# A transformer step on one core: the layout of an intermediate in DRAM, the place of 24 row gathers, and the place of eight gate products

## The chip, the cores and the metric

The kernel runs on one core of a Trainium2 chip. The metric is the device time of one execution in microseconds (us). The engines named below are PE (matrix products, with PEld for its weight loads), DVE (VectorE), ACT (ScalarE), POOL (GpSimd, which here issues the indirect gathers) and SP (SyncE, which issues nearly all other transfers).

## What is computed

One decoder layer in float32 on 512 prompt tokens and 64 decode tokens of width 1024: attention and a state-space branch are mixed by two gates, projected and normalised; then follows a layer of 16384 one-neuron experts (PEER) of which each token uses 8 x 16. The places that matter here:

```python
mix = jax.nn.sigmoid(ga) * (a @ w_attn_proj) + jax.nn.sigmoid(gb) * (s @ w_ssm_proj)
x = layer_norm(DN_ALPHA * x + mix @ w_out, ln1_g, ln1_b)
x = layer_norm(DN_ALPHA * x + peer(x, ...), ln2_g, ln2_b)
x = x + jax.nn.sigmoid(x @ ple_w_gate) * (p @ ple_w_proj)
# peer, one block of 128 tokens: 16 expert numbers idx and weights g for each of 8 heads
ue = u_tab[idx]
ve = v_tab[idx]
h = jax.nn.gelu(jnp.einsum('td,thkd->thk', xb, ue), approximate=False)
return jnp.einsum('thk,thkd->td', (g * h), ve)
```

## The kernel before

The tokens are five blocks: block 0 holds the 64 decode tokens, blocks 1 to 4 the prompt. Two groups run through the mixing one after the other: A (blocks 0 and 1, until about 397 us) and B (blocks 2 to 4, 384 token columns).

**PEER in two ways.** Blocks 2, 3 and 4 are computed densely over all 16384 experts, which are 128 columns of 128. `first` (L1202) makes 50 columns of activations: `up` (L1125) loads 512 KB of `u_t`, splits them on ACT (`uh`) and DVE (`ul`) into two parts and runs 24 matmuls (L1138) into `gl`; 48 of the results go to DRAM (`Hd`). Beside the columns runs `side`: the top-k of a block and then its `grid` (L1143), which turns the 128 weights of each token into a dense grid. A grid takes eight steps of 16 tokens; in each, DVE makes the tiles `o`, `eq`, `oa` and in most steps `ob` (ACT makes the others), PE multiplies them (L1169, L1170), ACT copies PSUM into `Gs`, and every second step a 2 MB `Gs` tile goes to `Gg` in DRAM (L1174), four times in a grid; there are two `Gs` tiles (`GSB`). `dense` (L1228) then walks over the 128 columns, the other 78 with their `up`, the last 50 with `gl` read back from `Hd`. Each column reads `v_tab` (512 KB), each fourth column four columns of the grid (`G<-Gg`, L1258, 768 KB), multiplies grid and activation (`wt`), splits both and runs the products of L1278. While the last 50 columns run, `w_gate` is loaded (`fr`) for the end of the program.

**Rows.** Blocks 1 and 0 are computed by gathers: `gathered_rows` (L1071) takes, for each of 128 (64 for block 0, packed) choices, one row of `u_tab` for every token, multiplies it with x on DVE and sums (`scr`, L1085), then the same with `v_tab` into `acc` (L1094). These are 384 rows: 192 of u, 192 of v. Each is one indirect gather of 512 KB issued by POOL (L1075) into one of four buffers `g`, and one DVE instruction. DVE keeps the rows in program order. The order is: u and v of block 1, then u and v of block 0. The gather for a row is issued when a buffer is free, so four run ahead of DVE.

**What sets the order.** Work is written as generators. At fixed places the code calls `pull(n)`, which adds n to an account and puts as many whole rows there: `PULL1` after each column of `first`, `PULL3` and `PULL4` in `dense`, `P0`, `P1`, `P2`, `P3`, `P4`, `PG` in group B's steps. What is left at the end of the program is done by `pull(1000)` ahead of block 0's layer norm. A scheduler then orders the instructions of each engine, within the bounds of data and buffers.

**Group B's mixing.** After the GLU of the state-space branch come `gate1` (L545: the eight gates of the second branch, 8 x 8 matmuls of L404, kept in `g1`), `mix0` (L561: attention times `w_ap` by L411, added into `mixB` by DVE), `mix1` (L575: state-space result times `w_sp`, times its gate, plus `mixB`), then `out`, `ln1`, `peerq`. Beside `mix0` DVE finishes the top-k of block 0 (tiles `eq`, `PF`, `ef`, `idx`), on which the first gathers of block 0 rest; the rows that are done there are block 1's.

**The end.** Block 0 comes last: after its last `acc` row a matmul folds it (L1100), DVE adds and normalises it, and PE runs its last gate products (L1373).

## Time and profile before

| | us |
|---|---|
| runs of the kernel before (3) | 1905.57, 1906.43, 1909.03; median 1906.43 |
| profiled execution, its own time | 1906.19 |
| its span in the profile | 1904.2 |
| group B from the GLU's end to `out` | 397 to 487 |
| `first`, 50 columns with three grids | from about 629, the last 242 us of it 690 to 932 |
| `dense`, 78 columns with `up` | 932 to 1563 |
| `dense`, last 50 columns | 1563 to 1799 |
| the end | 1799 to 1904.2 |

In the rows below, a table of windows gives for each stretch its length, the busy time of each engine with its number of instructions, the granted clock of TensorE as a share of full speed, the mean busy share of 16 DMA engines, and GB/s. A row of grouped instructions gives line, engine, operation, out<-in, count, then busy us and mean ns of one, then the idle time of the engine ahead of them and what ended it. A row of the timeline gives start, length, engine and line, and in brackets the idle time just ahead. Times are of one execution, from the start of its span.

### The profile page before, as it was taken

How to read it: one execution, taken by the hardware profiler on the slowest of the kernel's cores; microseconds unless marked ns; L12 is line 12 of the kernel's file. 1: busy time of each engine (PE TensorE's matmuls, PEld its weight loads, DVE VectorE, ACT ScalarE, POOL GpSimd, SP SyncE). 2: the span in 40 equal slices, each digit the busy share in tenths (PEclk: the TensorE clock that was granted, in tenths of full speed). 3: DMA queues.
4: the chain of work that ended last, by engine and by line, in shares of the span. 5: the costliest groups of instructions: out<-in, count | busy, mean ns of one | idle time of the engine just before them, and what ended most of it. 6: DMA issues, size and time to landing. Idle time of an engine off the chain costs nothing.

```text
span 1904.2 us, 26616 instructions
## 1 busy us (share of the span) xinstructions
PE 1789.2 (94%) x9506; PEld 1538.8 (81%) x9506; DVE 1474.5 (77%) x2969; ACT 770.0 (40%) x1145; POOL 576.4 (30%) x425
## 2 busy tenths in 40 slices
PE   7889999997999989999999999999999998999946
PEld 5768987756769678889999999999999996788835
DVE  7642344897889998968688888888888877988884
ACT  2115452241243259687733333333333324433311
POOL 4210000024431000000055555555555552332250
PEclk9899999998999989999999999999999999999978
DMA  7925464158794447577899999999999989999672
GB/s 215 305 91 171 148 221 167 55 190 330 272 358 168 136 159 283 196 282 267 310 375 367 348 335 350 336 352 333 353 337 342 342 285 410 392 353 355 215 235 85
DMA packets 211076, 515.45 MB, mean 271 GB/s; under 512 B 33536, under 2 KB 103184, under 8 KB 208880
## 3 DMA queue, kind: packets, MB, share of 16 engines
q1 hardware_dynamic: 144496, 301.68, 45.1%
q0 software_dynamic: 56160, 204.78, 29.3%
q10 hardware_dynamic: 10288, 7.30, 1.3%
q8 instruction: 74, 1.21, 0.2%
q14 instruction: 58, 0.48, 0.1%
HBM read 463.31 MB, written 51.89 MB: 271 GB/s over the span
## 4 chain that ended last, share of the span: by engine, by line
PE 63%; DVE 16%; DMA 9%; issue 6%; ACT 4%; POOL 1%; SPq 0%; ACTq 0%; DVEq 0%; POOLq 0%
PE psB L1278 11%; PE psA L1278 11%; PE psA L1138 11%; PE psB L1138 9%; PE psA L404 6%; PE psA L411 3%; DVE eq L217 3%; DMA g<-u_tab,idx 3%; ACT Gs L211 2%; PE psB L404 2%; DMA fr<-w_gate 2%; DMA g<-v_tab,idx 1%; POOL g L1075 1%; DVE scr L1085 1%; PE psA L648 1%
## 5 line engine op out<-in xcount | busy, mean ns | idle before, releaser
L1075 POOL DMA_INDIRECT g<-u_tab,idx x192 | 263.3, 1371 | 856.1 <-DVE scr L1085 571.2
L1075 POOL DMA_INDIRECT g<-v_tab,idx x192 | 274.2, 1428 | 315.3 <-DVE acc L1094 259.3
L1085 DVE SCALAR_TENSOR_TENSOR scr<-g,x 128x1024 bf16<-128x1024 f32 x192 | 234.6, 1222 | 38.3 <-DMA g<-u_tab,idx 36.7
L1094 DVE SCALAR_TENSOR_TENSOR acc<-g,hh,acc 128x1024 f32<-128x1024 f32 x190 | 243.6, 1282 | 15.9 <-DMA g<-v_tab,idx 13.9
L214 ACT ACTIVATE uh<-ur 128x1024 fp32r<-128x1024 f32 x120 | 127.2, 1066 | 138.3 <-PE psA L1138 70.2
L217 DVE TENSOR_TENSOR ul<-ur,uh 128x1024 fp32r<-128x1024 f32 x120 | 146.2, 1220 | 43.9 <-ACT uh L214 29.9
L214 ACT ACTIVATE vh<-vr 128x1024 fp32r<-128x1024 f32 x128 | 136.0, 1063 | 105.1 <-PE psB L1278 90.0
L214 ACT ACTIVATE wh<-wt 128x384 fp32r<-128x384 f32 x128 | 67.1, 524 | 239.2 <-PE psB L1278 221.8
L217 DVE TENSOR_TENSOR vl<-vr,vh 128x1024 fp32r<-128x1024 f32 x128 | 156.2, 1220 | 5.6 <-ACT vh L214 5.6
L1278 PE MATMUL psA<-vh,wh 128*128 128x512 f32 x384 | 150.4, 392 | 8.6 <-ACT wh L214 8.6
L217 DVE TENSOR_TENSOR wl<-wt,wh 128x384 fp32r<-128x384 f32 x128 | 71.6, 559 | 105.7 <-PE psB L1278 96.7
L1278 PE MATMUL psA<-vl,wh 128*128 128x512 f32 x384 | 150.9, 393 | 0.1
L1278 PE MATMUL psB<-vl,wh 128*128 128x512 f32 x384 | 150.6, 392 | 0.0
L1278 PE MATMUL psB<-vh,wh 128*128 128x512 f32 x384 | 150.2, 391 | 0.0
L1278 PE MATMUL psB<-vh,wl 128*128 128x512 f32 x384 | 149.9, 390 | 0.0
L1278 PE MATMUL psA<-vh,wl 128*128 128x512 f32 x384 | 149.5, 389 | 0.0
L1138 PE MATMUL psA<-xh,uh 128*128 128x384 f32 x648 | 135.3, 348 | 8.0 <-ACT uh L214 8.0
L404 PE MATMUL psB<-xTB,w 128*128 128x384 f32 x400 | 134.2, 492 | 5.9 <-ACT ev L214 5.9
L1138 PEld LDWEIGHTS psA<-xh,uh 128*128 128x128 f32 x648 | 115.7, 193 | 14.6 <-ACT uh L214 11.0
L1138 PE MATMUL psA<-xh,ul 128*128 128x384 f32 x648 | 127.1, 338 | 0.0
L1138 PE MATMUL psA<-xl,uh 128*128 128x384 f32 x648 | 126.9, 337 | 0.0
L404 PEld LDWEIGHTS psB<-xTB,w 128*128 128x128 f32 x400 | 76.3, 193 | 56.6 <-ACT ev L214 6.5
(366 smaller groups left out, 3625.2 us busy)
## 6 DMA issues: line engine op xcount, KB each, us to landing
ur<-u_t SPq DMA_DIRECT2D x128, 512.0 KB, 6.8
vr<-v_tab SPq DMA_DIRECT2D x128, 512.0 KB, 6.4
G<-Gg SPq DMA_DIRECT2D x33, 768.0 KB, 8.2
Gg<-Gs SPq DMA_DIRECT2D x12, 2048.0 KB, 7.4
w<-w_in SPq DMA_DIRECT2D x42, 512.0 KB, 5.2
w<-w_q SPq DMA_DIRECT2D x32, 512.0 KB, 5.3
Hd<-gl SPq DMA_DIRECT2D x48, 192.0 KB, 2.2
gl<-Hd SPq DMA_DIRECT2D x48, 192.0 KB, 5.6
```

The lines of the kernel that those rows point to most:

```text
L211: S.activation(out, in_, fn, **k)
L214: S.activation(out, in_, AF.Copy)
L217: return (e or V).tensor_tensor(out, a, b, op=op)
L404: T.matmul(out, w[:, k, :], x[:, k, :], start=(k == 0), stop=(k == kc - 1))
L411: T.matmul(out, a[:, k], b[:, k], start=f and k == 0, stop=l and k == kc - 1)
L648: T.matmul(p[bi][:n], a[:, k + i, c0:c0 + n], b[:, i], start=f and i == 0, stop=e and i == 1)
L1075: G.indirect_dma_start(out=t, out_offset=None, in_=I[tab], in_offset=bass.IndirectOffsetOnAxis(ap=IDX[bi][:, i:i + 1], axis=0))
L1085: pin(V.scalar_tensor_tensor(scr, t, 1.0, X1[bi], op0=mult, op1=mult, accum_out=hh[:, i:i + 1]))
L1094: pin(V.scalar_tensor_tensor(acc, t, hh[:, i:i + 1], acc, op0=mult, op1=add))
L1138: T.matmul(p, w[:, c * 128:c * 128 + 128], z[:, c], start=f and c == 0, stop=l and c == 7)
L1278: T.matmul(y[b][hf], x[:, bs], z[:, hf * 512:hf * 512 + 512], start=f, stop=l)
```

## The change

Four things change.

1. `Gg` is laid out in DRAM as [128, 32, 12, 128] in place of [12, 128, 128, 32]. A write of `Gs` (2 MB) now consists of 4096 pieces of 512 bytes, where it was 128 pieces of 16 KB; a read of four columns (768 KB) consists of 128 pieces of 6 KB, where it was 1536 pieces of 512 bytes.
2. `PULL1` goes from 0.25 to 0.75, `P0` from 1 to 0.75, `P1` from 0.5 to 1.5, and the 16 rows of `gate1` (`PG`) fall away.
3. `gate1` is gone; `mix1` computes each gate of B itself, as it did for group A, between its products.
4. `up` is cut into `up_parts` (load and split) and `up` (matmuls); in `first` the parts of the next column stand ahead of the matmuls of this one.

```diff
--- before.py
+++ after.py
@@ -37,7 +37,7 @@
 E0 = 50
 EB, KB, TB = 1, 1, 1
 BQ, ABG, AB0, AB1, AB2 = 2, 0, 1, 1.5, 2
-P0, P1, P2, P3, P4, PG = 1, 0.5, 3, 2, 2, 2
+P0, P1, P2, P3, P4 = 0.75, 1.5, 3, 2, 2
 YFIRST = True
 QK0, QK1 = (4, 0, 1), (2, 3)
 SIDE = 2
@@ -54,7 +54,7 @@
 T0, T1, T2 = 0.5, 1, 1
 LATE = 0
 AHEAD = 3
-PULL1, PULL3, PULL4, PULL5 = 0.25, 3, 1, 2
+PULL1, PULL3, PULL4, PULL5 = 0.75, 3, 1, 2
 
 
 
@@ -542,13 +542,6 @@
                             act(g.mx[:, n], g.mm(g.ln.wload(I["w_in"][10 + n]), g.xT, 8), AF.Sigmoid)
                             yield
 
-                    def gate1(g, xp):
-
-                        g.g1 = xp.tile([128, 8, g.N], FP, name="g1", tag="xh")
-                        for n in range(8):
-                            act(g.g1[:, n], g.mm(g.ln.wload(I["w_in"][18 + n]), g.xT, 8), AF.Sigmoid)
-                            yield
-
                     def half(g, w, n, x):
 
                         o = n % 2 * 4
@@ -586,11 +579,8 @@
                             if n % 2 == 0:
                                 w = l.wload(I["w_sp"][n // 2])
                                 w = w if g.first else parts(w)
-                            if g.first:
-                                t = l.ev(g.N)
-                                act(t, g.mm(l.wload(I["w_in"][18 + n]), g.xT, 8), AF.Sigmoid)
-                            else:
-                                t = g.g1[:, n]
+                            t = l.ev(g.N)
+                            act(t, g.mm(l.wload(I["w_in"][18 + n]), g.xT, 8), AF.Sigmoid)
                             tt(t, g.half(w, n, x), t, mult)
                             tt(t, g.mx[:, n], t, add)
                             copy(g.mh[:, n], t)
@@ -1112,7 +1102,7 @@
                 while rows and next(rows[0], rows) is rows:
                     rows.pop(0)
 
-        Gg = dp.tile([12, 128, 128, 32], FP, name="Gg")
+        Gg = dp.tile([128, 32, 12, 128], FP, name="Gg")
         Hd = dp.tile([E0, 128, 384], FP, name="Hd")
 
         def split(pool, raw, cols, tags, bufs):
@@ -1122,17 +1112,20 @@
             tt(lo, raw, hi.bitcast(FP), sub)
             return hi, lo
 
-        def up(e2, x, du, hp, tag="gl", bufs=5, whole=False, deep=3, lanes="AB"):
+        def up_parts(e2, du, whole=False, deep=3):
 
             raw = du.tile([128, D], FP, tag="ur", name="ur", bufs=3)
             SY.dma_start(raw, I["u_t"][e2].rearrange("p c e -> p (c e)"))
+            return (raw,) if whole else split(du, raw, D, "u", deep)
+
+        def up(e2, u, x, hp, tag="gl", bufs=5, lanes="AB"):
+
             xh, xl, xr = x
             p = ps(384, lanes[e2 % len(lanes)])
-            if whole:
-                terms = ((raw, xr, True, True),)
+            if len(u) == 1:
+                terms = ((u[0], xr, True, True),)
             else:
-                hi, lo = split(du, raw, D, "u", deep)
-                terms = ((hi, xh, True, False), (hi, xl, False, False), (lo, xh, False, True))
+                terms = ((u[0], xh, True, False), (u[0], xl, False, False), (u[1], xh, False, True))
             for w, z, f, l in terms:
                 for c in range(8):
                     T.matmul(p, w[:, c * 128:c * 128 + 128], z[:, c], start=f and c == 0, stop=l and c == 7)
@@ -1171,7 +1164,7 @@
                     o = t0 % 32 + u
                     act(Gs[:, :, o:o + 4].rearrange("p e t -> p t e"), p, AF.Copy, scale=1.0 / GSC)
                 if t0 % 32 == 16:
-                    SY.dma_start(Gg[b * 4 + t0 // 32], Gs)
+                    SY.dma_start(Gg[:, :, b * 4 + t0 // 32], Gs.rearrange("p (q e) t -> p q (e t)", e=4))
 
             st, late = {}, None
             for t0 in range(0, 128, 16):
@@ -1214,12 +1207,17 @@
                     yield from grid(b, oh, io16)
 
             work = side()
+            def parts_of(e2):
+                return up_parts(e2, du, W0 <= e2 < W1, DEEP)
+
+
+            u = parts_of(0)
             for e2 in range(E0):
-                how = dict(whole=W0 <= e2 < W1, deep=DEEP, lanes="A")
+                u, now = parts_of(e2 + 1) if e2 + 1 < E0 else None, u
                 if e2 < KEEP:
-                    H0[e2] = up(e2, x, du, hp, "keep", KEEP, **how)
+                    H0[e2] = up(e2, now, x, hp, "keep", KEEP, lanes="A")
                 else:
-                    SY.dma_start(Hd[e2], up(e2, x, du, hp, **how))
+                    SY.dma_start(Hd[e2], up(e2, now, x, hp, lanes="A"))
                 for _ in range(SIDE):
                     next(work, 0)
                 pull(PULL1)
@@ -1239,7 +1237,7 @@
                     if n == 128 - E0:
                         st["end"] = last()
                     if e2 >= E0:
-                        H[n] = up(e2, xs, du, hp)
+                        H[n] = up(e2, up_parts(e2, du), xs, hp)
                     elif e2 < KEEP:
                         H[n] = H0[e2]
                     else:
@@ -1255,7 +1253,7 @@
                     SY.dma_start(vraw, I["v_tab"].rearrange("(a b) d -> b a d", b=128)[e2])
                     if n == 0 or e2 % 4 == 0:
                         gt_ = dv.tile([128, 12, 4, 32], FP, tag="G", name="G", bufs=2)
-                        SY.dma_start(gt_, Gg[:, :, e2 - e2 % 4:e2 - e2 % 4 + 4].rearrange("b p e t -> p b e t"))
+                        SY.dma_start(gt_.rearrange("p b e t -> p (b e t)"), Gg[:, e2 // 4].rearrange("p b c -> p (b c)"))
                     w = dv.tile([128, 384], FP, tag="wt", name="wt", bufs=WTB)
                     tt(w.rearrange("p (b t) -> p b t", b=12), gt_[:, :, e2 % 4], H.pop(n).rearrange("p (b t) -> p b t", b=12), mult)
                     wh, wl = split(dv, w, 384, "w", WTB)
@@ -1494,8 +1492,6 @@
         beside(B.gate(), T0)
         B.load_y()
         beside(B.glu(), T1)
-        for _ in B.gate1(xp):
-            pull(PG)
         wH1 = ExitStack()
         ws["H"] = open_(wH1, "wH1", 4, "right")
         for _ in B.mix0(xp):
```

Counted in DVE's order of both programs, the rows done by certain places are:

| rows done (of 384) | before | after |
|---|---|---|
| start of `out` of group B | 27 | 16 |
| end of group B's layer norm | 44 | 34 |
| first split of a column in `first` | 63 | 54 |
| first split of a `v_tab` column in `dense` | 73 | 88 |
| first sum after `dense` (L1292) | 357 | 372 |
| the last run of rows ahead of L1101 | 17 | 2 |

So 10 fewer rows stand ahead of `first`, 24 more in it (34 for 10), as many as before in `dense`, and 15 fewer behind it. Within each of the three grids there are now six rows and seven columns' splits beside thirty tiles of the grid; before, two rows were in each.

DVE in group B's mixing, ahead of the first sums into `mixB`, before (`scr` are rows, `wl` a split weight):

```order
L1085 SCALAR_TENSOR_TENSOR scr_3210,hh_3067<-g_3208,x1_1_2017 128x1024
L1085 SCALAR_TENSOR_TENSOR scr_3214,hh_3067<-g_3212,x1_1_2017 128x1024
L1085 SCALAR_TENSOR_TENSOR scr_3249,hh_3067<-g_3247,x1_1_2017 128x1024
L1085 SCALAR_TENSOR_TENSOR scr_3270,hh_3067<-g_3268,x1_1_2017 128x1024
L1085 SCALAR_TENSOR_TENSOR scr_3307,hh_3067<-g_3305,x1_1_2017 128x1024
L217 TENSOR_TENSOR mixB_2824<-psB_3228,mixB_2824 128x384
L217 TENSOR_TENSOR mixB_2824<-psB_3251,mixB_2824 128x384
L217 TENSOR_TENSOR wl_3330<-w_3327,wh_3329 128x1024
```

And after (`eq`, `ef` belong to the top-k of block 0):

```order
L217 TENSOR_TENSOR eq_3011<-eq_3011,CI_2959 64x1664
L217 TENSOR_TENSOR wl_3110<-w_3107,wh_3109 128x1024
L217 TENSOR_TENSOR eq_3011<-eq_3011 64x32x26
L217 TENSOR_TENSOR mixB_2824<-psB_3065,mixB_2824 128x384
L217 TENSOR_TENSOR eq_3011<-eq_3011 64x32x13
L217 TENSOR_TENSOR mixB_2824<-psB_3084,mixB_2824 128x384
L1006 TENSOR_REDUCE ef_2962<-eq_3011 64x32
L217 TENSOR_TENSOR mixB_2824<-psB_3113,mixB_2824 128x384
L217 TENSOR_TENSOR eq_3037<-PFx_3038,iota16_143 64x1664
```

The rows ahead of `mixB` are gone; what stands between its sums now is the top-k.

DVE in the first grid, from its second step, before:

```order
L217 TENSOR_TENSOR o1_5455<-e1T_5366,io16_5028 128x2048
L217 TENSOR_TENSOR eq_5456<-e2T_5367,io16_5028 128x2048
L217 TENSOR_TENSOR ul_5512<-ur_5508,uh_5511 128x1024
L217 TENSOR_TENSOR oa_5457<-eq_5456,gh_5368 128x2048
L217 TENSOR_TENSOR ob_5458<-eq_5456,gl_5369 128x2048
L1085 SCALAR_TENSOR_TENSOR scr_5506,hh_3067<-g_5504,x1_1_2017 128x1024
L217 TENSOR_TENSOR o1_5542<-e1T_5366,io16_5028 128x2048
L217 TENSOR_TENSOR eq_5543<-e2T_5367,io16_5028 128x2048
```

And after:

```order
L1075 SCALAR_TENSOR_TENSOR scr_5416,hh_3102<-g_5414,x1_1_2017 128x1024
L217 TENSOR_TENSOR ul_5421<-ur_5418,uh_5420 128x1024
L217 TENSOR_TENSOR o1_5452<-e1T_5355,io16_4995 128x2048
L217 TENSOR_TENSOR eq_5453<-e2T_5356,io16_4995 128x2048
L217 TENSOR_TENSOR ul_5508<-ur_5505,uh_5507 128x1024
L217 TENSOR_TENSOR oa_5454<-eq_5453,gh_5357 128x2048
L217 TENSOR_TENSOR ob_5455<-eq_5453,gl_5358 128x2048
L1075 SCALAR_TENSOR_TENSOR scr_5503,hh_3102<-g_5501,x1_1_2017 128x1024
L217 TENSOR_TENSOR o1_5539<-e1T_5355,io16_4995 128x2048
L217 TENSOR_TENSOR eq_5540<-e2T_5356,io16_4995 128x2048
```

Rows now stand between the tiles of the grid's steps at about every second step or closer.

DVE at the end of the program, ahead of block 0's fold (L1101, in the changed kernel L1091), before:

```order
L1065 SCALAR_TENSOR_TENSOR x_4_14654<-x_4_14654,rs,nb 128x1024
L1094 SCALAR_TENSOR_TENSOR acc<-g,hh,acc 128x1024
L217 TENSOR_TENSOR sgm<-sgm,po 128x512
L217 TENSOR_TENSOR x_3_14617<-x_3_14617,sgm 128x512
L1094 SCALAR_TENSOR_TENSOR acc<-g,hh,acc 128x1024 x17
L1101 SCALAR_TENSOR_TENSOR x_0_2015<-x_0_2015,psB 128x512 x2
```

And after:

```order
L1055 SCALAR_TENSOR_TENSOR x_4_14706<-x_4_14706,rs,nb 128x1024
L1084 SCALAR_TENSOR_TENSOR acc<-g,hh,acc 128x1024
L217 TENSOR_TENSOR sgm<-sgm,po 128x512
L217 TENSOR_TENSOR x_3_14669<-x_3_14669,sgm 128x512
L1084 SCALAR_TENSOR_TENSOR acc<-g,hh,acc 128x1024 x2
L1091 SCALAR_TENSOR_TENSOR x_0_2015<-x_0_2015,psB 128x512 x2
```

The run of 17 rows that closed the program is one of two.

## Rows read from the trace of the kernel before

**Rows 1.** Page, first part: busy us, share and instructions of each engine.
```profile
PE 1789.2 (94%) x9506; PEld 1538.8 (81%) x9506; DVE 1474.5 (77%) x2969; ACT 770.0 (40%) x1145; POOL 576.4 (30%) x425
```

**Rows 2.** Table of windows by stage: length, engines, PEclk, DMA share, GB/s.
```profile
397.00:439.00 42.00, 42.00 (x133) 24.91 (x132) 37.49 (x89) 15.42 (x20) 19.57 (x14) 1.00 0.70 242
439.00:487.00 48.00, 35.57 (x192) 35.28 (x191) 35.62 (x60) 10.43 (x14) 16.16 (x16) 0.86 0.86 325
...
690.00:932.00 242.00, 229.07 (x1727) 213.90 (x1726) 200.29 (x297) 193.33 (x291) 15.48 (x10) 0.97 0.68 248
932.00:1563.00 631.00, 631.00 (x3226) 578.36 (x3226) 525.55 (x633) 239.82 (x308) 342.84 (x226) 1.00 0.95 343
1563.00:1799.00 236.00, 226.92 (x986) 185.80 (x986) 199.58 (x268) 91.75 (x118) 64.81 (x59) 0.99 0.95 350
```

**Rows 3.** The end: timeline of PE, then of DVE, then one group (1833 to 1904.2).
```profile
1865.45 3.78 PE L1100 MATMUL psB<-acc,c_fold 128*128 128x512 f32 x4 [30.79 <-DVE acc L1094]
...
1869.73 2.76 PE L1373 MATMUL psB<-w_gateh,th 128*128 128x512 f32 x8
...
1886.85 1.98 PE L1373 MATMUL psA<-w_gateh,th 128*128 128x512 f32 x8
...
1835.78 1.28 DVE L1094 SCALAR_TENSOR_TENSOR acc<-g,hh,acc 128x1024 f32<-128x1024 f32 x1 [1.38 <-DMA g<-v_tab,idx]
...
1864.11 1.28 DVE L1094 SCALAR_TENSOR_TENSOR acc<-g,hh,acc 128x1024 f32<-128x1024 f32 x1 [0.56 <-DMA g<-v_tab,idx]
...
L1094 DVE SCALAR_TENSOR_TENSOR acc<-g,hh,acc 128x1024 f32<-128x1024 f32 x17 | 21.9, 1286 | 10.4 <-DMA g<-v_tab,idx 9.9 <-DVE acc L1094 0.3
```

**Rows 4.** Group B's mixing: timeline of PE; group of DVE's rows, 397 to 439.
```profile
397.23 41.44 PE L404 MATMUL psB<-xTB,w 128*128 128x384 f32 x128
...
459.43 2.90 PE L411 MATMUL psB<-at,wh 128*128 128x384 f32 x8 [12.43 <-DVE mixB L217]
...
L1085 DVE SCALAR_TENSOR_TENSOR scr<-g,x 128x1024 bf16<-128x1024 f32 x12 | 14.6, 1219 | 3.9 <-DMA g<-u_tab,idx 3.8
```

**Rows 5.** `first`, 690 to 932: groups of instructions; last, one line's min/median/max ns.
```profile
L217 DVE TENSOR_TENSOR ul<-ur,uh 128x1024 fp32r<-128x1024 f32 x43 | 52.4, 1223 | 36.4 <-ACT uh L214 29.9 <-PE psA L1138 6.4
...
L1085 DVE SCALAR_TENSOR_TENSOR scr<-g,x 128x1024 bf16<-128x1024 f32 x10 | 12.2, 1223 | 0.0
...
L1085 DVE DVE_READ_ACCUMULATOR scr<-g,x x10: 82/86/95, 712.5 to 921.1; 128x1 f32 x10
```

**Rows 6.** Table of windows within `first`: the three grids and two stretches ahead of them.
```profile
690.00:703.00 13.00, 11.47 (x67) 11.21 (x66) 12.88 (x27) 10.70 (x14) 0.00 (x0) 1.00 0.53 180
703.00:762.00 59.00, 56.37 (x455) 51.65 (x455) 51.81 (x66) 51.01 (x80) 4.37 (x3) 0.94 0.66 246
762.00:790.00 28.00, 27.21 (x158) 26.85 (x157) 27.69 (x97) 17.20 (x19) 1.68 (x1) 1.00 0.69 232
790.00:844.00 54.00, 46.83 (x404) 41.15 (x403) 47.73 (x50) 44.27 (x73) 4.40 (x3) 0.97 0.57 214
...
873.00:932.00 59.00, 58.20 (x488) 54.48 (x487) 49.84 (x53) 54.14 (x85) 5.04 (x3) 1.00 0.73 266
```

**Rows 7.** DMA issues: out<-in, count, KB each, median us to landing; then L1258 (reads of G).
```profile
vr<-v_tab SPq DMA_DIRECT2D x128, 512.0 KB, 6.4
G<-Gg SPq DMA_DIRECT2D x33, 768.0 KB, 8.2
Gg<-Gs SPq DMA_DIRECT2D x12, 2048.0 KB, 7.4
...
Hd<-gl SPq DMA_DIRECT2D x48, 192.0 KB, 2.2
...
DMA to landing us min/median/max: 5.2/8.2/12.3
```

**Rows 8.** Last 50 columns: the window where PE waits most; reads of G, 1563:1663.
```profile
1583.00:1603.00 20.00, 15.44 (x60) 11.92 (x59) 16.14 (x25) 5.59 (x7) 6.39 (x6) 0.91 1.04 409
...
L1258 SPq DMA_DIRECT2D G<-Gg x6: 421/434/1262, 1574.7 to 1661.0; - x6
```

## The prediction

> **What bounds the kernel now.** I read the page's first part, then a table of windows by stage, then in each stage what ended the idle time of PE. PE is busy 94% of the span [rows 1], so a gain can lie only where PE waits or runs at the lower clock. By stages [rows 2]: from 932 to 1563 PE is busy 631.0 of 631.0 us; no transfer, row or layout is worth anything there as long as that cover holds. In group B's mixing PE is busy 35.6 of 48 us after the gates; in `first` 229.1 of 242; in the last 50 columns 226.9 of 236. The largest single wait is at the end [rows 3]: PE sits idle 30.79 us ahead of the fold L1100, released by DVE's `acc`. There 17 rows stand in a run, and DVE isn't slow either: they are 21.9 us of work with 10.4 us of idle, nearly all of it for the gathers. Nothing else is left to do then.
>
> **The end: 15 rows fewer.** Of the 17 rows two remain, and the rows ahead of them in the last stage are as many as before. The second row now starts at 1835.78 and ends at 1837.06; the seventeenth starts at 1864.11 and ends at 1865.39 [rows 3]. What follows hangs on the last row alone, so it moves by 28.3 us; I take 28. After the long idle time L1373's first eight matmuls took 2.76 us, later ones 1.98, and the fold's four took 3.78 [rows 3]; with an idle time of some 2 us in place of 31 this slow start should mostly go, about 1 us. **−29 us**, between −27 and −31. What the 15 rows cost where they are done instead is the rest of the sum.
>
> **Group B's mixing.** `gate1` is 128 matmuls in an unbroken 41.44 us [rows 4]; the same products now run in `mix1`, so PE's work is unchanged: 42.0 + 35.6 = 77.6 us of the 90 [rows 2]. The 12.4 us of idle are one wait: PE stands 12.43 us at 459.43 for DVE's `mixB` [rows 4], which is queued behind the rows, and the granted clock over this window is 0.86 [rows 2]. The ten rows taken from ahead of `first` leave this place, so that wait goes. What is late next: without the gates `mix0` comes 41 us earlier, into DVE's top-k of block 0, where DVE was busy 37.5 of 42 us [rows 2]. Of these the twelve rows, 14.6 + 1.0 us [rows 4, 5], go away; eight sums into `mixB` (384 wide against a row's 1024, so an estimate of 0.5 us each) and two more splits (1.22, as `ul` [rows 5]) come, which makes 28 us. Beside that PE has half of 35.6, or 18 us, of `mix0` and one gate (5.2) that the order puts there: 23 us, so 5 us of idle, or 14 if the waits of the two engines for each other stretch it to the old 37.5. I take 10, against 12.4, and 1 us for the clock: **−3 us**, between −12 (PE never waits) and +6 (the old 37.5 with the gate not yet there). The gates' ACT work and weight loads move with them and are covered by the products they now stand between.
>
> **`first`: the rows.** 24 more rows are 24 x (1.223 + 0.086) = 31 us of DVE [rows 5]; the second summand is the read of the sum behind each row. DVE is busy 200.3 of 242 [rows 2], and of its idle time 36.4 us lie ahead of `ul` [rows 5], that is, it waits for the column's first part, not for rows: the ten rows that are there waited 0.0 us. Splitting a column ahead takes just this wait away, since the parts no longer stand behind the matmuls of the column before. So the rows would fill it, but to 232 of 242. The nearest rows for a DVE that is full are two short stretches [rows 6]: 690 to 703 (12.88 of 13, PE 11.47, 88%) and 762 to 790 (27.69 of 28, PE 27.21, 97%). PE's 229 us at 97% are 236, at 88% 260. Bounds 0 to +18; I take **+5**, nearer to the longer stretch. The gathers are POOL's; it was busy 15.5 us of the 242 [rows 2], so their issue costs nothing.
>
> **`first`: writes of G.** Twelve writes of 2 MB took 7.4 us each in 16 KB pieces [rows 7]; in 512-byte pieces none is shown. The nearest rows are the reads of G, 1536 such pieces: 5.2 us at best, 8.2 in the median. With 2.2 us of fixed time (a 192 KB write of `Hd` takes that) 4096 pieces come to 2.2 + 4096/1536 x 3.0 = 10.2 us, or with 6.0 to 18.2. So a write costs +2.8 to +10.8 us of the DMA engines. I take +4, near the low end, because the median is from a stage whose DMA share was 0.95 and more [rows 2], so it holds the waiting for other transfers. Alone that is hidden by the second `Gs` tile. But together it is not small: the three grids have DMA shares of 0.66, 0.57 and 0.73 over 59, 54 and 59 us [rows 6], or 39, 31 and 43 us; each gets 4 x 4 = 16 us of writes and four more gathers at 512 KB, 1.3 us each at the 400 GB/s of the fullest windows [rows 8]. That makes 60, 52 and 64 us: 1, 0 and 5 over. With the last write, which the first read of `dense` waits for, landing some 3 us later: **+8 us**. At +2.8 it is 1; at +10.8 the grids need 87, 79 and 91, which is +85.
>
> The Trainium skill, "DMA: Bandwidth & Descriptors", section Specifications, puts the size from which a transfer runs at line rate at 512 B; by that rule the writes cost nothing extra, this term is 0 and the sum 8 us lower. The trace shows no write that decides it; its reads of G at 8.2 us for 768 KB against 6.4 for 512 KB of `v_tab` in 4 KB pieces [rows 7] don't speak against the rule.
>
> **`dense`.** 932 to 1563 is bound by PE alone: 0. In the last 50 columns DMA binds where PE waits: in the fullest 20 us its share is 1.04 and PE is busy 15.4 [rows 8]. A read of G in 6 KB pieces should cost the best price of long pieces, 2.2 + 768/2048 x 5.2 = 4.2 us in place of 5.2. Six such reads are issued from 1563 to 1663 [rows 8], so up to −6 where all is bound by transfers; half of the time is: **−3 us**, from −6 to 0. The 15 rows done earlier don't thin out the gathers there, since as many stand in `dense` as before.
>
> The same page, section Latency and other measured facts, has copies slow down when rows lie 2 MB apart (164 against 207 GB/s at 512 KB), as the twelve blocks of the old layout do; by that the reads would gain 20% or so and the term come to about −8. The rate per KB of these reads is no worse than that of `v_tab` [rows 7], so no such loss shows here.
>
> **Sum** against the profiled execution (1906.2, which is 0.2 below the median): −29 − 3 + 5 + 8 − 3 = −22, **1884 us**.
>
> **Rivals.**
> (a) *`first` takes the rows and the writes for nothing.* For: `ul` waits 36.4 us, DMA is at 0.68. Then −29 − 3 + 0 + 1 − 3 = −34: 1872 us.
> (b) *The grids become bound by transfers, and `first` gives most of the gain back.* For: 0.73 in the third grid already. A write at +5.5 us: 4 x 5.5 + 5 = 27 more per grid, so 66, 58, 70, that is 7 + 4 + 11 = 22, with the last landing 25, rows +6: 1906 − 29 − 3 + 31 − 3 = 1902 us.
> (c) *Slower: the 512-byte writes cost as much as the median read of G.* +85 in the grids: 1906 − 29 − 3 + 5 + 85 − 3 = 1961 us. Above about +6 us a write (13.4 to landing) the change is a loss: each further us adds twelve. Against it: the minimum of 5.2 shows that the price is not in the pieces.
> (d) *The wait in the mixing only changes its name*, top-k in place of rows, and it is longer: +6 in place of −3, 1893 us.
> That rows don't get earlier can't be: DVE keeps them in program order, and the order shows 372 of 384 ahead of the end.
>
> **How the numbers follow.** Forecast (1877 to 1891) 0.50; (a) 0.18; (b) 0.14; (c) 0.10; (d) 0.08. A measurement can tell about 0.2% (4 us) from no change. Faster: the forecast, (a), (d) and somewhat under half of (b), 0.82; within 0.2%: the middle of (b), 0.07; slower: (c) and the rest of (b), 0.11. The range reaches from below (a), where the mixing also gains 5, to the upper end of (b): 1867 to 1907. What is left out is (c) above all, and a little at either end.
>
> **What would show it.** At the end: PE's idle time ahead of the fold at 2 to 4 us and two rows behind the last others. In the mixing: no wait for `mixB` behind rows, but several of 1 to 3 us in the top-k's time, and `out` starting near 485. In `first`: `ul` waiting far less for `uh`, 34 rows, DVE at 230 us, a length of 250 to 260 from 690's place on; `Gg` at 10 to 13 us to landing; if ACT's `Gs` begins to wait for a transfer, (b) or (c) holds. In the last 50 columns: reads of G at 7 us or less and `w_gate` as late as before. The forecast is wrong if `first` grows by over 30 us, or if a wait of PE shows in 932 to 1563.

## The result

The changed kernel takes 1879.4 us (median of four runs, 1878.45 to 1880.87) against 1906.36 for the kernel before: a ratio of 0.9857, 95% interval 0.984 to 0.9874. The forecast was 1884 us, 5 us above. One execution of the changed kernel in a later series took 5025.6 us; it is left out, and that series' median below is of the other three.

Where the time went is read from fixed marks in both traces: the start of the last matmul of `yTB` (end of the GLU), the first product of `out`, the first matmul of `first`, the issue of the first read of G, the issue of the first read of `Hd`, the end. Lengths in us:

| stage | before | after | difference |
|---|---|---|---|
| start to the GLU's end (nothing changed there) | 396.9 | 400.3 | +3.4 |
| mixing, to the first product of `out` | 90.1 | 85.8 | −4.3 |
| `out`, `ln1`, `peerq`, to the first matmul of `first` | 148.6 | 154.3 | +5.7 |
| `first`, to the first read of G | 303.7 | 306.2 | +2.5 |
| `dense`, 78 columns, to the first read of `Hd` | 625.3 | 623.0 | −2.3 |
| last 50 columns and the end | 339.6 | 307.9 | −31.7 |

The two reads are issued ahead of PE's work with them, so these marks part `first` from the 78 columns only roughly. Taken from PE's first product of `dense` instead (L1278, after the change L1276), `first` is 2.8 us shorter and the 78 columns are 3.7 us longer; in a second execution of the changed kernel the two differences are +0.1 and +3.9. Together both stages take 0.2 us more by the table and 1.0 by PE, in the second execution 3.2 and 4.0.

The page of the kernel after shows that PE does the same work in a shorter span (its counterpart is [rows 1]):

```profile
PE 1789.9 (95%) x9506; PEld 1534.5 (82%) x9506; DVE 1470.9 (78%) x2969; ACT 770.4 (41%) x1145; POOL 594.6 (32%) x425
```

**The end.** The timeline of PE, and the groups of 1799 to 1877.5, answer to [rows 3]:

```profile
1834.40 1.11 PE L1358 MATMUL psA<-c_ident,x 128*128 128x128 f32 x4 [2.81 <-DVE x L1055]
1836.26 2.07 PE L1371 MATMUL psA<-w_gateh,th 128*128 128x512 f32 x4 [0.75 <-ACT th L214]
1839.43 3.78 PE L1090 MATMUL psB<-acc,c_fold 128*128 128x512 f32 x4 [1.10 <-DVE acc L1084]
...
L1084 DVE SCALAR_TENSOR_TENSOR acc<-g,hh,acc 128x1024 f32<-128x1024 f32 x12 | 15.4, 1281 | 0.1
```

The wait of 30.79 us ahead of the fold is 1.10. The fold stands 36.8 us behind the last product of `dense` (1802.6) where it stood 66.5 behind (1798.9); what follows it takes 38.1 in place of 38.8. The rows no longer wait for their gathers (0.1 us of idle for twelve).

The fold itself takes 3.78 us in both kernels, and the granted clock over it is 0.50 in both, the lower level of 1.2 GHz. In the kernel before PE had stood for 30.79 us. In the kernel after it had worked without a wait until 1831.6, then stood for 2.81 us, and the clock is 0.50 from 1834.3 on. The row of the table of windows over the fold after the change:

```profile
1839.43:1843.21 3.78, 3.78 (x5) 1.61 (x6) 0.69 (x1) 0.00 (x0) 0.00 (x0) 0.50 0.02 4
```

**Mixing.** PE's timeline, for [rows 4]:

```profile
407.70 1.01 PE L411 MATMUL psB<-at,wh 128*128 128x384 f32 x2 [4.13 <-ACT wh L214]
410.57 2.93 PE L411 MATMUL psB<-at,wl 128*128 128x384 f32 x8 [1.86 <-DVE wl L217]
...
439.88 0.96 PE L411 MATMUL psB<-st,wl 128*128 128x384 f32 x4 [1.22 <-DVE wl L217]
```

The one wait of 12.43 us is three, 7.2 us together. Behind it, in `out` (L638, before L648), PE waits longer for split weights than it did. In PE's waits from 486 to 640 (us in total, times, longest) there are, before the change and after it,

```profile
PE psB L648 <- DVE wl L217: 2.7, 1, 2.7
...
PE psA L648 <- DVE wl L217: 1.9, 1, 1.9
```

```profile
PE psA L638 <- DVE wl L217: 6.6, 1, 6.6
```

**`first`.** The stretch 690 to 932 of the table of windows, for [rows 2], 30 us of its second grid, then two groups of the whole stretch, for [rows 5]:

```profile
690.00:932.00 242.00, 229.51 (x1722) 212.36 (x1722) 230.28 (x376) 191.41 (x280) 50.84 (x33) 0.98 0.85 286
...
820.00:850.00 30.00, 29.40 (x242) 26.70 (x240) 26.81 (x54) 28.72 (x44) 5.04 (x3) 1.00 0.99 337
...
L217 DVE TENSOR_TENSOR ul<-ur,uh 128x1024 fp32r<-128x1024 f32 x42 | 51.4, 1224 | 11.4 <-ACT uh L214 11.4
...
L1075 DVE SCALAR_TENSOR_TENSOR scr<-g,x 128x1024 bf16<-128x1024 f32 x33 | 40.3, 1222 | 0.0
```

DVE is 30 us busier in the same 242 us and PE is as busy as before; the wait ahead of `ul` has shrunk from 36.4 us to 11.4; the rows wait for nothing. The DMA share is 0.85 for 0.68. In the stage behind it PE no longer works all the time: the row for 932 to 1563, which in [rows 2] has 631.00 of 631, is now

```profile
932.00:1563.00 631.00, 628.38 (x3214) 574.54 (x3213) 523.18 (x631) 242.57 (x319) 339.09 (x227) 1.00 0.94 347
```

PE waits there twice for `ul`, at 971 and 981, in the first columns of `dense`: 2.5 us in all.

**Transfers of G.** The page's DMA issues, median us to landing, for [rows 7], and the reads' least, median and longest:

```profile
G<-Gg SPq DMA_DIRECT2D x33, 768.0 KB, 7.7
Gg<-Gs SPq DMA_DIRECT2D x12, 2048.0 KB, 9.0
...
DMA to landing us min/median/max: 6.0/7.7/12.8
```

A write in 512-byte pieces takes 1.6 us more to landing than one in 16 KB pieces (7.4), a read in 6 KB pieces 0.5 us less than before. These medians are over the transfers whose landing the trace tells: 5 writes of 12 after and 4 before, 16 reads of 33 in each.

What the pieces cost the DMA engines can be summed from every packet of the traces. The twelve writes before are 1536 packets of 644 ns on average, which is 5.2 us of all 16 engines for each write; after they are 49152 packets of 27 ns, 6.9 us for each. The 33 reads go the other way: 2.7 us of the engines for one in 512-byte pieces, 2.0 in 6 KB pieces. So the writes cost the engines 21 us more in all, and the reads 22 less.

### The profile page after: what moved, and what is told of

Same layout as the page of the kernel before. It is cut to its first block, busy times and chain, and to the rows that moved or that the text cites. A ratio compares the mean times of both kernels' runs of the same rounds, so it can differ in the third digit from the quotient of the medians.

```text
span 1877.5 us, 26587 instructions
## 1 busy us (share of the span) xinstructions
PE 1789.9 (95%) x9506; PEld 1534.5 (82%) x9506; DVE 1470.9 (78%) x2969; ACT 770.4 (41%) x1145; POOL 594.6 (32%) x425
## 4 chain that ended last, share of the span: by engine, by line
PE 63%; DVE 13%; issue 8%; DMA 8%; ACT 4%; POOL 2%; SPq 0%; ACTq 0%; DVEq 0%; POOLq 0%
PE psB L1276 12%; PE psA L1276 12%; PE psA L1131 10%; PE psB L1131 7%; PE psA L404 6%; DMA g<-u_tab,idx 4%; PE psA L411 3%; PE psB L404 3%; POOL g L1065 2%; DVE eq L217 2%; ACT Gs L211 2%; PE psA L638 1%; DVE scr L1075 1%; DMA fr<-w_gate 1%; DVE ul L217 1%
## 5 line engine op out<-in xcount | busy, mean ns | idle before, releaser
L1065 POOL DMA_INDIRECT g<-u_tab,idx x192 | 272.8, 1421 | 794.3 <-DVE scr L1075 487.7
L1065 POOL DMA_INDIRECT g<-v_tab,idx x192 | 283.2, 1475 | 326.0 <-DVE acc L1084 276.6
L1075 DVE SCALAR_TENSOR_TENSOR scr<-g,x 128x1024 bf16<-128x1024 f32 x192 | 234.5, 1222 | 30.3 <-DMA g<-u_tab,idx 29.4
L1276 PE MATMUL psA<-vh,wh 128*128 128x512 f32 x384 | 150.3, 391 | 8.2 <-ACT wh L214 8.2
L1276 PE MATMUL psB<-vl,wh 128*128 128x512 f32 x384 | 151.1, 393 | 0.0
L1276 PE MATMUL psA<-vl,wh 128*128 128x512 f32 x384 | 150.9, 393 | 0.0
L1276 PE MATMUL psB<-vh,wl 128*128 128x512 f32 x384 | 150.1, 391 | 0.0
L1276 PE MATMUL psB<-vh,wh 128*128 128x512 f32 x384 | 150.1, 391 | 0.0
L1276 PE MATMUL psA<-vh,wl 128*128 128x512 f32 x384 | 149.7, 390 | 0.0
L1131 PE MATMUL psA<-xh,ul 128*128 128x384 f32 x648 | 133.9, 344 | 4.4 <-DVE ul L217 4.3
L1131 PEld LDWEIGHTS psA<-xh,ul 128*128 128x128 f32 x648 | 114.4, 191 | 7.7 <-DVE ul L217 5.9
```

What stands on the lines that cost most here:

```text
L1065: G.indirect_dma_start(out=t, out_offset=None, in_=I[tab], in_offset=bass.IndirectOffsetOnAxis(ap=IDX[bi][:, i:i + 1], axis=0))
L1075: pin(V.scalar_tensor_tensor(scr, t, 1.0, X1[bi], op0=mult, op1=mult, accum_out=hh[:, i:i + 1]))
L1131: T.matmul(p, w[:, c * 128:c * 128 + 128], z[:, c], start=f and c == 0, stop=l and c == 7)
L1276: T.matmul(y[b][hf], x[:, bs], z[:, hf * 512:hf * 512 + 512], start=f, stop=l)
```

## The experiments

The rows below are lengths by the same marks, as differences from the profiled execution of the kernel before, and the measured ratio. "Gates" is the stretch of the mixing. Each row is one profiled execution and not always one near the median: that of the last kernel is 1893.5 us of a median of 1902.1, that with 256-byte pieces 1939.5 of 1931.4.

| kernel | gates | `out` to `first` | `first` | 78 columns | last 50 and end | ratio |
|---|---|---|---|---|---|---|
| changed kernel | −4.3 | +5.7 | +2.5 | −2.3 | −31.7 | 0.9857 |
| the same again | −3.8 | +3.5 | +5.1 | −1.9 | −30.7 | 0.9856 |
| changed, old layout | −4.7 | +3.4 | +2.7 | +1.8 | −29.3 | 0.9853 |
| before, new layout | +0.2 | +4.4 | +1.2 | −1.2 | +0.7 | 0.9994 |
| changed, parts not ahead | −5.1 | +3.4 | +9.3 | −1.1 | −32.3 | 0.9887 |
| changed, gates apart | −1.7 | +0.7 | +4.7 | −2.1 | −38.4 | 0.983 |
| before, more rows | −2.2 | +0.6 | +6.7 | +0.1 | −37.8 | 0.9839 |
| changed, few rows | −5.0 | +3.0 | −0.8 | −0.2 | +17.3 | 1.0065 |
| changed, still more rows | −5.0 | −2.9 | +20.5 | −0.3 | −30.3 | 0.9924 |
| changed, 256-byte pieces | −4.6 | +2.2 | +54.8 | +2.0 | −31.0 | 1.0105 |
| 12 more rows in 78 columns | −5.4 | +2.7 | +4.5 | +0.2 | −41.3 | 0.9817 |
| the same, 8 of them from `out` | −5.3 | −3.6 | +5.0 | −1.2 | −37.2 | 0.9797 |
| 36 more rows in 78 columns | −5.3 | −3.6 | +1.3 | +23.9 | −31.7 | 0.9963 |

The first stretch, up to the GLU's end, in which no kernel differs, varied from +0.8 to +9.6 us. So a difference of some 3 us in one stage of one execution says little; the larger ones are what follows rests on.

### The layout of G, taken out and put in alone

```diff
-        Gg = dp.tile([128, 32, 12, 128], FP, name="Gg")
+        Gg = dp.tile([12, 128, 128, 32], FP, name="Gg")
```

with the write and the read as in the kernel before; and the other way round in the kernel before. In both pairs PE, DVE and ACT run their instructions in the same order with either layout, so that nothing but the transfers differs.

> The changed kernel with the old layout of G in DRAM (writes of 16 KB pieces, reads of 512-byte pieces); rows, gates and column order as changed. Theory 1 (the forecast's terms: the small write pieces cost `first` something through the DMA engines, the long read pieces give some back in the last 50 columns): `first` gets 3 to 8 us shorter, the last 50 columns 1 to 3 us longer, 1874 to 1878 us in all against 1879.4. Rival 2 (writes are hidden behind the second tile, only the reads count): `first` stays, the last 50 columns are 2 to 5 us longer, 1881 to 1884. Rival 3 (the layout is neutral): 1879 within 2.

> The kernel before with the new layout of G alone; 10 rows in `first`, so the DMA engines have room there (share 0.68). Theory 1 (the write's pieces cost only where the DMA engines are full): `first` stays within 2 us, the last 50 columns gain 1 to 3: 1903 to 1907 us. Rival 2 (the writes lengthen the grids by themselves): `first` 4 to 8 us longer, 1908 to 1913.

Ratios 0.9853 (0.9832 to 0.9874) and 0.9994 (0.998 to 1.0009): with the rest of the change or without it, the layout moves nothing that can be measured. For the changed kernel the third theory holds (its median in that series was 1883.3, but the kernel before was slower in it too, 1910.7); for the kernel before the first one, without the gain in the last columns. `first` was +2.7 with the old layout and +2.5 and +5.1 with the new, and +1.2 in the kernel before. In the packets of these two traces the writes show the same prices as in the pair above, 5.2 us of the 16 engines for each in the old layout and 6.9 in the new, and the reads 2.7 and 2.1. So a write costs the engines 1.7 to 1.8 us more, where the forecast had 4, and nobody waits for it.

### The rows alone, fewer of them, more of them

```diff
-PULL1, PULL3, PULL4, PULL5 = 0.25, 3, 1, 2
+PULL1, PULL3, PULL4, PULL5 = 0.75, 3, 1, 2
```

in the kernel before and nothing else; 0.25 in the changed kernel; and in the changed kernel `PULL1` 1 with `P4` 1.

> The kernel before with 25 more rows in `first` and nothing else (no run of rows is left at the end of the program). Theory 1 (the rows that leave the end are the whole gain, and `first` has room for them): the end 29 to 32 us shorter, `first` 2 to 12 us longer, 1878 to 1888 us. Rival 2 (`first` has no room without the parts one column ahead): `first` 15 to 30 us longer, 1892 to 1905.

The kernel before with more rows in `first` has a ratio of 0.9839 (0.9815 to 0.9862), 1879.9 us: as much as the whole change. Since its mixing still holds ten more rows, no run of them is left for the end, and the end is 38 us shorter, where 29 to 32 were expected and the changed kernel has 32. `first` costs it 6.7 us. So the first theory holds but for the size of the end, and the rows that leave the end carry the gain by themselves.

> The changed kernel with 10 rows in `first` in place of 34, and so 27 in a run at the end in place of 2. Theory 1 (each row of that run costs 1.9 us of the end, and the rows in `first` cost 2 to 5 us together): the end 47 us longer, `first` 2 to 5 shorter, 1921 to 1925 us. Rival 2 (the rows beside the grids cost `first` more, hidden in the forecast's surplus): `first` 8 us or more shorter, 1918 or less.

1922.7 us, ratio 1.0065 (1.0045 to 1.0086): the first theory. PE's wait for the fold, with 27 rows in the run:

```profile
1883.75 3.78 PE L1090 MATMUL psB<-acc,c_fold 128*128 128x512 f32 x4 [49.04 <-DVE acc L1084]
```

From 27 rows to two, the last stretch differs by 17.3 + 31.7 = 49 us, 1.96 for each row, and `first` gives up 3 to 6 us for 23 rows.

> The changed kernel with 45 rows in `first` (a full one per column) and 8 in place of 16 in group B's `out`; one row is left at the end. Theory 1 (in `out` PE waits behind rows that wait for their gathers, and `first` has room left): from the start of `out` to `first` 2 to 5 us less, the end 1 to 2 less, `first` 0 to 4 more: 1874 to 1879 us. Rival 2 (DVE in `first` is full with 34 rows, 230 of 242 us): `first` 8 us or more longer, 1882 or more.

For `first` the second theory holds: it is 20.5 us longer than before, ratio 0.9924 (0.9905 to 0.9944), 1894.3 us. From `out` to `first` the kernel does take less, as the first one said, 6 to 9 us less than the changed kernel (2 to 5 expected). In the table of windows DVE is full wherever a grid runs; one of these windows:

```profile
810.00:840.00 30.00, 25.02 (x213) 21.61 (x212) 30.00 (x52) 24.91 (x40) 8.08 (x5) 1.00 1.07 354
```

PE is busy 25 of 30 us beside a DVE that is busy all the time. The DMA share there is over 1 as well, so that this one run doesn't say which of the two decides. The price isn't proportional: the first 24 rows cost about 4 us, the next 11 some 16.

### The column's parts one column ahead

```diff
-                u, now = parts_of(e2 + 1) if e2 + 1 < E0 else None, u
+                now = parts_of(e2)
```

> The changed kernel with each column's load and split in `first` standing right ahead of its own matmuls again, all else as changed; DVE has the 24 further rows in `first` all the same. Theory 1 (the parts one column ahead take away DVE's wait for the first part, which was 36.4 us before and is 11.4 after, and so make the room for the rows): that wait comes back to 25 us or more, `first` is 6 to 15 us longer, 1885 to 1894 us. Rival 2 (PE is the bound of `first` and the order does nothing): 1879 within 3, with the wait for the first part back or not.

1888.6 us, ratio 0.9887 (0.9865 to 0.9909), in the same series in which the changed kernel with the old layout had 0.9853: 6.5 us, with `first` at +9.3 for +2.5 to +5.1. DVE's wait, by the waits of `first` (us in total, times, longest):

```profile
DVE ul L217 <- ACT uh L214: 21.6, 7, 7.4
```

It comes back to 21.6 us, less than the 25 expected. In the kernel before with more rows, where the parts aren't ahead either, it is 20.2 us and `first` costs 6.7. The time went as the first theory said, but its reason doesn't hold. In the changed kernel with few rows the parts do stand one column ahead, and the wait is what it was before the change (36.4 us). The group of 690 to 932 there:

```profile
L217 DVE TENSOR_TENSOR ul<-ur,uh 128x1024 fp32r<-128x1024 f32 x43 | 52.2, 1220 | 37.3 <-ACT uh L214 37.3
```

So the parts ahead don't take the wait away. It is DVE's spare time, and rows fill it: the further rows in `first` bring it from 36 down to 20 us without the parts ahead, and from 37 to 11 with them. What the parts ahead give is that the rows fit in better. That is worth some 3 to 6 us beside the many rows; beside few, `first` is 0.8 us shorter than before, which is within the spread.

### The gates as a stage of their own

The function `gate1` and its loop as before, `P0, P1 = 1, 0.5`, in the changed kernel.

> The changed kernel with the eight gates of group B as a stage of their own again, and the rows beside them as in the kernel before; layout, column order and the more rows in `first` as changed. 10 more rows stand ahead of `first` by this, so that none is left for the end. Theory 1 (the gates' place gained 4 us in the mixing, which the longer wait in `out` took back; the two last rows at the end are worth 3): mixing 3 to 5 us longer to the start of `out`, 4 to 6 us less from there to `first`, the end 2 to 3 less: 1875 to 1880 us. Rival 2 (the gates between the products are a gain of their own): 1882 to 1887.

1876.1 us, ratio 0.983 (0.9808 to 0.9851): by its time the first theory, though the mixing is only 2 to 3 us longer (3 to 5 expected) and the end gains more than was expected. The gates between the products make the mixing about 3 us shorter, −3.8 to −5.4 in ten executions against −2.2 to +0.2 in those with the gates apart. From `out` to `first` the order is turned round: +2.2 to +5.7 with the gates between the products and all 16 rows in `out`, and 0.0, +0.6, +0.7 and +4.4 with the gates apart. Together they are worth nothing that these runs can tell. What the gates apart do change is that ten more rows fit ahead of `first`, and the end is 6.7 us shorter for it, where 2 to 3 were expected. The two last rows alone are not the reason. From the last product of `dense` on, PE runs 277 matmuls in either kernel. In the changed kernel they take 64.3 us at a mean granted clock of 0.92, and PE waits 4.7 us between them (2.81, 0.75 and 1.10 above); with the gates apart they take 59.7 us at 0.98, and PE waits for nothing.

### Pieces of 256 bytes

```diff
-        Gg = dp.tile([128, 32, 12, 128], FP, name="Gg")
+        Gg = dp.tile([128, 64, 12, 64], FP, name="Gg")
```

with the write in 8192 pieces and the tile of the read turned to match (one piece of 6 KB per partition).

> The changed kernel with G in groups of two columns: each write is 8192 pieces of 256 bytes, each read again one piece of 6 KB per partition. Theory 1 (each further piece costs what the step from 128 to 4096 pieces did, 1.6 us to landing for 3968): writes land in 10.5 to 11 us, `first` is 0 to 5 us longer, 1879 to 1885. Rival 2 (pieces under 512 bytes cost much more than by their number): writes land in 15 us or more, ACT's copies into the tile begin to wait for the write, `first` 15 us or more longer, 1895 or more.

1931.4 us, with `first` 54.8 us longer. By its numbers this is the second theory, but the run doesn't show it: this kernel also runs its instructions in another order. The scheduler put the first grid's later steps ahead of the columns' splits that had stood between them, and the top-k of the third block into the middle of the second grid, whose first write was issued at 837.3 in place of 808.0. After the change 68 us from the first write hold 65.8 us of PE at a clock of 0.97; here 66 us hold 46.8 at 0.80. So the run doesn't tell what the pieces cost in time. What they cost the DMA engines its packets tell: 98304 of 18 ns, 9.2 us for each write, where it was 6.9 in 512-byte pieces. The last packet of a write ended 12.9 us after the issue (median of twelve), against 8.2 to 8.9 in ten executions with 512-byte pieces. That lies between the two theories (10.5 to 11 us to landing, and 15 or more).

### More rows where PE has cover

In the changed kernel, with `P4` and `PULL1` as the text on each says:

```diff
-PULL1, PULL3, PULL4, PULL5 = 0.75, 3, 1, 2
+PULL1, PULL3, PULL4, PULL5 = 0.75, 3.16, 1, 2
```

> The changed kernel with 12 more rows in the 78 columns of `dense` (PULL3 3.16 for 3), so that no row is left behind `dense`; the 12 that stood there were ten between the last steps and two in the last run. Theory 1 (the rows behind `dense` still cost 6.7 us, as the kernel with its gates apart showed, and PE covers rows in the 78 columns for nothing): `dense` within 1 us, the end 5 to 8 us shorter, 1872 to 1876 us. Rival 2 (transfers fill there, share 0.94, and PE begins to wait): `dense` 5 us or more longer, 1879 or more.

> The same with 8 of the 16 rows of group B's `out` moved to the 78 columns of `dense` too (P4 1 for 2, PULL3 3.27). Theory 1 (the rows in `out` hold up the splits that PE waits for): from the start of `out` to `first` 5 to 9 us less than in the changed kernel, `dense` within 2, the end 5 to 8 less, 1862 to 1870 us. Rival 2 (PE's wait in `out` is for something else): `out` to `first` within 3, 1871 or more.

> As before, with 12 of the 16 rows of `out` and 12 of the 34 of `first` moved to the 78 columns of `dense` (P4 0.5, PULL1 0.5, PULL3 3.49; 38 more rows there than in the changed kernel). Theory 1 (PE's cover in `dense` is not used up): `out` to `first` 6 to 10 us less, `first` 1 to 4 less, the end 5 to 8 less, `dense` within 3: 1858 to 1867 us. Rival 2 (38 x 1.3 us of gathers at 400 GB/s are 50 us, and `dense` at a share of 0.94 has 37 of its 625 us free): `dense` 8 us or more longer, 1868 or more.

> The changed kernel once more, on the same chip as these three, to compare them with, and to see what a stage varies by where nothing is changed: the first 397 us and the stretch from `out` to `first`. If the 5.7 us by which that stretch was longer belong to the change, they are there again (4 to 7); if they are of that one execution, 0 to 3. The ratio to before 0.984 to 0.987.

In this series the changed kernel had a ratio of 0.9856 (0.9818 to 0.9893), 1879.5 us. With twelve more rows in the 78 columns: 1871.7 us, 0.9817 (0.9791 to 0.9844). The last stretch is 10 us shorter still (expected 5 to 8), since no row is left in a run behind `dense`, and the 78 columns are +0.2, 2 us more than in the changed kernel (expected within 1). With eight rows of `out` there too: 1868.6 us, 0.9797 (0.977 to 0.9824), the fastest of all by its median and ahead of both kernels; from the one with twelve rows its interval doesn't part it. From `out` to `first` it takes 7 to 9 us less than the changed kernel, and the wait of L638 for `wl` is gone from its waits; the 78 columns are 1 us longer than in the changed kernel. Both first theories hold in the main. With 36 more in all (the text above counts 38; DVE's order has 36) the cover gives out: +23.9 us in the 78 columns, ratio 0.9963 (0.9947 to 0.9979), the second theory. The table of windows of the 78 columns, for the second and the third of these (the kernel before: 631.0 busy of 631, share 0.95, 343 GB/s in [rows 2]):

```profile
938.00:1562.00 624.00, 620.04 (x3157) 566.33 (x3157) 548.23 (x668) 236.55 (x306) 357.76 (x247) 1.00 0.97 363
```

```profile
934.00:1583.00 649.00, 637.36 (x3223) 576.98 (x3222) 565.09 (x699) 220.33 (x308) 387.48 (x262) 1.00 0.97 359
```

and the waits there of the third (us in total, times, longest):

```profile
ACT wh L214 <- DVE wt L217: 283.0, 55, 9.0
...
DVE acc L1084 <- DMA g<-v_tab,idx: 39.9, 33, 3.3
DVE scr L1075 <- DMA g<-u_tab,idx: 37.1, 38, 2.4
```

The rows now wait 77 us for their gathers, DVE holds `wt` behind them, ACT waits for that, and PE for the splits behind it: 9.8 us of PE's waits in this window are for `wl`. From PE's first product of `dense` to that of the 79th column it is 655.2 us, with PE idle for 17.2, against 631.6 and 2.5 in the changed kernel and 634.8 and 4.0 with 20 rows more. At 363 GB/s nearly all was still covered; with 16 more rows than that the transfers don't come faster (359) and the rest waits.

The same kernel run again shows +3.5 from `out` to `first` in place of +5.7, just under what was expected of a cost of the change; five other kernels with the gates between the products and 16 rows in `out` show +2.2 to +3.4. But the kernel before with the new layout, where nothing differs there, shows +4.4. So a wait in `out` is real (L638 waits in one piece 5.7 to 6.8 us in the seven executions with the gates between the products and 16 rows in `out`, and not in those with 8 rows or fewer), but that the stretch as a whole is longer by more than 2 us is not settled.

## Why the prediction was right, and where it was not

- **The end, −29.** It moved by 30.4 us: the fold came 29.7 us closer to the last product (forecast 28), since the rows that are left no longer wait for gathers either, and 0.7 us were gained behind it (forecast 1). The mechanism was right, the size to within 2 us. The reason given for the 1 us was not: the fold did not get faster with the shorter idle time. It takes 3.78 us in both kernels, at the lower clock in both, and 1.88 only in kernels where PE comes to it without a wait (below).
- **Mixing, −3.** −4.3 and −3.8. As said, the wait for `mixB` behind the rows went and smaller waits took its place, 7.2 us where the forecast had 10. What the step didn't see is that rows and splits in `out` would be late next: the rival (d), a wait that only changes its name, came true one stage further on, with 6.6 us at L638 where 4.6 stood before. That stretch is 3.5 and 5.7 us longer in two executions, of which no more than some 2 us are shown to belong to the change.
- **`first`, the rows, +5.** With the layout's share at nothing, `first` cost +2.5 and +5.1; two further executions of the same order show +2.7 and +4.5. The size was right, and DVE went to 230 us, as said. The reason was right in half: the rows filled the idle time ahead of `ul`, but the parts one column ahead did not take it away, since with few rows it is 37.3 us with them. The room ends soon after these rows.
- **`first`, the writes of G, +8.** This step failed. It was mis-sized at two places. The price of a write was bounded from below by +2.8 us, from reads in a busier stage, and taken as +4; it is +1.6 to landing, and 1.8 of the DMA engines' time. And the grids were counted as if they had to hold their own transfers; in the second grid of the kernel after a share of 0.99 over 30 us stands beside a PE busy 29.4 of them (the second row of `first` above). Two pairs of kernels with equal order put the term at nothing. The sum of the step has a slip too: 1, 0 and 5 us over and 3 for the last landing are 9, not 8, and the ends of its range leave the landing out. The Trainium skill, "DMA: Bandwidth & Descriptors", section Specifications, puts line rate at 512 B and above; by that the term was 0, as the time shows it. For the rate itself this case's traces don't agree: 2 MB took the engines 6.9 us in 512-byte pieces and 5.2 in 16 KB pieces.
- **`dense`, 0 and −3.** −2.3 and −1.3. The sign that would make the forecast wrong, a wait of PE in 932 to 1563, did show, with 2.5 us. For the last columns no effect of the layout can be told: the reads cost the DMA engines 0.7 us less each, 8 us for the twelve issued there, but their median to landing there is 7.6 us for 7.2, and the last stretch is 1.4 to 2.4 us shorter with the new layout in one pair and 0.7 longer in the other. The Trainium skill, "DMA: Bandwidth & Descriptors", section Latency and other measured facts, would have made the term −8 by its figure for rows 2 MB apart. That figure is for the distance from one partition's row to the next; here the blocks are 2 MB apart and the partitions 16 KB, and no run shows such a gain.
- **What nothing in the sum stands for.** `out`, `ln1` and `peerq` came out +5.7 us, and the stretch ahead of the GLU's end, where both programs are the same, +3.4 (in the second execution +3.5 and +0.8).
- **The sum.** That it came within 5 us is in part luck. `first` and the 78 columns together were forecast at +13 and came out at +0.2, so for them the rival (a) was nearer, and its 1872 us; the 9.1 us of the two stretches that the sum had no term for filled most of that gap. Of the other signs, the fold's wait came out shorter (1.10 for 2 to 4 us), `Gg` landed in 9.0 us for 10 to 13, the reads in 7.7 for 7 or less, and `first` grew to about 245 us for 250 to 260; `ul` waiting far less, 34 rows, DVE at 230 us and `out` at 486 came as said.

## What to carry to other kernels

Work left for the end of a program is paid in full there, here 1.9 us for each row of 1.28, gather wait and all; the same work costs next to nothing beside a stage that one engine fills, until the transfers of that stage are full too. Look for the last such stage first (here the 78 columns took 20 more rows for 1 to 3 us), then for one in which every engine has some room. Idle time ahead of an instruction tells how much room the engine has, and not that this instruction's place is the cause: here it went with the rows and not with the order of the parts. A change that moves several things should be taken apart: here one number, the rows for each column, had all the gain, and the layout none.

## What the runs showed of the hardware

- A 2 MB write to DRAM took the 16 DMA engines 5.2 us in 128 pieces of 16 KB, 6.9 in 4096 of 512 bytes and 9.2 in 8192 of 256 bytes (mean packet 644, 27 and 18 ns). A 768 KB read took them 2.7 us in pieces of 512 bytes and 2.0 in pieces of 6 KB. In the time of the program the step from 16 KB to 512 bytes was not seen (ratios 0.9994 and, the other way, 0.9853 for 0.9857).
- The same four matmuls of the fold took 3.78 us at a granted clock of 0.50, behind 1.1 to 49 us of idle, and 1.88 us at 1.00 where PE had worked without a wait ahead of them. The row of the table of windows over the fold in the kernel with its gates apart:

```profile
1810.31:1812.19 1.88, 1.88 (x7) 0.86 (x6) 1.68 (x5) 1.63 (x2) 0.00 (x0) 1.00 0.00 0
```

- In the 78 columns 363 GB/s were reached over 624 us with PE at work all but 4 us, and asking for more gave 359 and waits. In single windows of 20 us it was 409 [rows 8].
